# Pinned queue orders, half tiles for the sums of a step by seven, and a fourth such step in twelve gate/up groups of a two-layer decoder trunk

## The chip, the cores and the metric

The kernel runs on one core of one Trainium2 chip. The metric is device time in microseconds (us) of one execution. The core's engines, as the profile names them, are PE (TensorE, matmuls; PEld is its weight load), DVE (VectorE), ACT (ScalarE), POOL (GpSimd) and SP (SyncE, which here only starts transfers). Each works through a queue of its own in order.

## The reference

A decoder trunk of two layers on 256 tokens of width 2048, all in float32:

```python
h = x                                              # (1, 256, 2048)
for i in range(2):
    hn = rmsnorm(h, norm_mix[i])
    if i % 2 == 0:
        mix = pool_mixer(hn, pool_w[0], pool_scale[0])
    else:
        mix = diff_attention(hn, w_qkv[0], ..., w_o[0], lambda_init)
    h = h + mix
    h = h + swiglu(rmsnorm(h, norm_ffn[i]), w_gate[i], w_up[i], w_down[i])
return rmsnorm(h, final_norm)

def swiglu(h, wg, wu, wd):
    return (jax.nn.silu(h @ wg) * (h @ wu)) @ wd   # 2048 -> 5632 -> 2048
```

Nearly all arithmetic is in the products with `w_gate`, `w_up`, `w_down`, `w_qkv` and `w_o`.

## The kernel before, in words

**Stages.** A pooling mixer (the first 42 us of the trace), the FFN of layer 0 (to about 755 us), attention (to about 1085 us), the FFN of layer 1, and a last normalization. An FFN takes its 11 gate/up groups of 512 columns in chunks of 4, 4 and 3 (`CHUNKS`); behind each chunk come two down groups (`o` of 0 and 1) that add the chunk's share to the residual `x_tok`.

**A group and its steps.** `group` computes a 256 x 1024 block of results: 512 gate and 512 up columns, or 1024 columns of another product. It sums over *pairs* of 128 input rows: 8 pairs in a gate/up group, 8 or 6 in a down group. A pair is one step: one 1 MB load of four 128 x 512 weight blocks (B12, B11, B22, B21) into `raw`, which has three buffers. Float32 weights and operands are each split into a high and a low half of type fp32r, and a product of two blocks is three matmuls: high x high, high x low, low x high. ACT casts `whi` from `raw`, and VectorE subtracts to get `wlo` (`halves`); these too have three buffers each. The results lie in PSUM, one bank each of 128 x 512.

**Plain steps and steps by seven.** A plain step multiplies 2 x 2 blocks by 2 x 2 blocks in eight products, 24 matmuls. A step by seven uses Strassen's scheme (in Winograd's form): seven products, 21 matmuls, with four sums of weight blocks T1 to T4 (`sums` makes `tsum` on VectorE), which are split in their turn: `thi` by ACT, `tlo` by VectorE (`sum_halves`). The operand's sums S1 to S4 are made once, when it is transposed (`pair`), in a tile of eight blocks instead of four. Block B12 itself is not needed by such a step, so `halves` leaves it out (128 x 1536 instead of 128 x 2048). `SEVEN` names the pairs that go by seven in gate/up groups, (2, 4, 6), and in each layer's first group (4, 6). Down groups, the attention's q/k, v and output groups have tables of their own. The q/k and v groups take their pairs in the order `LATE`, with 4, 2 and 6 next to each other; their sums' halves have two buffers (`bufs=2`). In the FFN they have one.

**End of a group.** `combined` adds the seven banks up (one chain of ACT copies and eight VectorE additions named `c`), the gate half goes through SiLU on ACT, and `pair` transposes the result into an operand `h` of the down groups. The next group's first matmuls, meanwhile, are already running.

**What sets the order.** The code is written as a program for one thread. A scheduler orders each engine's queue by program order and by its own model of the engines; in two places of the pooling stage `high_priority` with a negative number moves work behind. Semaphores between the engines are derived from the tiles.

The lines of the profile before that matter: L189 the matmuls of a group, L124 and L125 the casts and subtractions of weights, L130, L132, L133 the sums, L139 and L140 their halves, L211 to L220 `combined`, L252 to L277 the operand's halves, L354 and L368 the pooling's weights and matmuls, L392 and L393 the pooling's residual.

The cut that both versions keep, of one product:

```python
for x, y in ((ah, hi), (ah, lo), (al, hi)):
    left[b] -= 1
    nc.tensor.matmul(ps[b], x, y[:, block], start=first, stop=(left[b] == 0))
```

## Time and profile before

| | |
|---|---|
| median of 3 runs | 1837.09 us (1836.84 to 1837.28) |
| the profiled execution's own time | 1837.09 us |
| its span, first to last instruction | 1835.3 us |
| busy: PE, PEld | 1823.0 us (99%), 1492.3 us (81%) |
| busy: DVE, ACT | 1630.5 us (89%), 1048.7 us (57%) |
| matmuls of L189 | 7,530 |
| steps, and steps by seven | 328 with a load, of them 114 by seven |
| loaded from HBM | 353 MB, 193 GB/s over the span |

How to read it: "busy" is the union of the times in which an engine had an instruction running. Matmuls overlap their neighbours, so one lasts 0.39 us in the records while the next starts 0.227 us after it; the pitch, not the duration, is what a matmul costs. A wait is written "waiter <- what it waited for". The clock column is the TensorE clock that was granted, 1.00 being full.

### The profile page before, as it was taken

How to read it: one execution, taken by the hardware profiler on the slowest of the kernel's cores; microseconds unless marked ns; L12 is line 12 of the kernel's file. 1: busy time of each engine (PE TensorE's matmuls, PEld its weight loads, DVE VectorE, ACT ScalarE, POOL GpSimd, SP SyncE). 2: the span in 40 equal slices, each digit the busy share in tenths (PEclk: the TensorE clock that was granted, in tenths of full speed). 3: DMA queues.
4: the chain of work that ended last, by engine and by line, in shares of the span. 5: the costliest groups of instructions: out<-in, count | busy, mean ns of one | idle time of the engine just before them, and what ended most of it. 6: DMA issues, size and time to landing. Idle time of an engine off the chain costs nothing.

```text
span 1835.3 us, 20926 instructions
## 1 busy us (share of the span) xinstructions
PE 1823.0 (99%) x8192; PEld 1492.3 (81%) x8192; DVE 1630.5 (89%) x1692; ACT 1048.7 (57%) x1026; POOL 0.7 (0%) x6
## 2 busy tenths in 40 slices
PE   9999999999999999999999999999999999999997
PEld 6888888888888888888888888888888888888886
DVE  7999999889899899989988789889899899988986
ACT  6655544555554556666667665555554555555563
POOL 0000000000000000000000000000000000000000
PEclk9999999999999999999999999999999999999999
DMA  7555555555555555544554555555555545556552
GB/s 271 200 184 193 208 196 209 204 187 205 205 194 197 205 184 184 206 173 174 182 183 163 181 184 184 206 185 205 204 190 202 207 183 193 212 215 210 202 189 110
DMA packets 50930, 356.35 MB, mean 194 GB/s; under 512 B 6160, under 2 KB 6288, under 8 KB 8464
## 3 DMA queue, kind: packets, MB, share of 16 engines
q1 hardware_dynamic: 49968, 353.40, 53.5%
q10 hardware_dynamic: 864, 1.63, 0.2%
q8 instruction: 64, 1.05, 0.2%
q14 instruction: 34, 0.28, 0.0%
HBM read 352.90 MB, written 2.10 MB: 193 GB/s over the span
## 4 chain that ended last, share of the span: by engine, by line
PE 97%; DVE 1%; ACT 1%; DMA 0%; issue 0%; SPq 0%; DVEq 0%; ACTq 0%
PE b L189 93%; PE b L259 2%; PE b L576 1%; PE b L607 0%; DMA x_tok<-x_n 0%; PE b L368 0%; PE b L624 0%; PE b L622 0%; PE b L623 0%; PE b L561 0%; DVE wlo L354 0%; DVE xt_hl L252 0%; ACT sq L240 0%; DVE wlo L125 0%; DVE z L392 0%
## 5 line engine op out<-in xcount | busy, mean ns | idle before, releaser
L189 PE MATMUL b<-whi,xp 128*128 128x512 f32 x2784 | 899.4, 392 | 0.0
L124 ACT CAST whi<-raw 128x1536 fp32r<-128x1536 f32 (+1 forms) x328 | 578.7, 1764 | 549.6 <-PE b L189 450.4
L125 DVE TENSOR_TENSOR wlo<-raw,whi 128x1536 fp32r<-128x1536 f32 (+1 forms) x328 | 689.6, 2103 | 159.2 <-ACT whi L124 158.9
L189 PEld LDWEIGHTS b<-whi,xp 128*128 128x128 f32 x2784 | 520.1, 188 | 108.2 <-ACT e L272 0.4
L189 PE MATMUL b<-wlo,xp 128*128 128x512 f32 x1392 | 544.2, 391 | 0.0
L189 PE MATMUL b<-whi,h 128*128 128x512 f32 x1108 | 354.2, 390 | 0.0
L189 PEld LDWEIGHTS b<-wlo,xp 128*128 128x128 f32 x1392 | 261.5, 188 | 53.0
L140 DVE TENSOR_TENSOR tlo<-tsum,thi 128x2048 fp32r<-128x2048 f32 x114 | 260.6, 2286 | 8.3 <-ACT thi L139 8.3
L189 PEld LDWEIGHTS b<-whi,h 128*128 128x128 f32 x1108 | 207.5, 188 | 43.2
L139 ACT CAST thi<-tsum 128x2048 fp32r<-128x2048 f32 x114 | 217.6, 1908 | 19.7 <-DVE tsum L133 17.2
L189 PE MATMUL b<-thi,xp 128*128 128x512 f32 x640 | 223.4, 389 | 0.0
L189 PE MATMUL b<-wlo,h 128*128 128x512 f32 x554 | 215.8, 389 | 0.0
L130 DVE TENSOR_TENSOR tsum<-raw 128x1024 f32<-128x1024 f32 x114 | 139.1, 1220 | 2.1 <-DMA raw<-w_v 0.6
L189 PEld LDWEIGHTS b<-thi,xp 128*128 128x128 f32 x640 | 120.1, 188 | 24.7
L189 PE MATMUL b<-tlo,xp 128*128 128x512 f32 x320 | 125.9, 393 | 0.0
L189 PEld LDWEIGHTS b<-wlo,h 128*128 128x128 f32 x554 | 104.0, 188 | 21.3
L189 PE MATMUL b<-thi,h 128*128 128x512 f32 x240 | 83.7, 390 | 0.0
L133 DVE TENSOR_TENSOR tsum<-tsum,raw 128x512 f32<-128x512 f32 x114 | 78.5, 689 | 2.2
L132 DVE TENSOR_TENSOR tsum<-tsum,raw 128x512 f32<-128x512 f32 x114 | 78.1, 685 | 0.6
L189 PEld LDWEIGHTS b<-tlo,xp 128*128 128x128 f32 x320 | 60.0, 188 | 16.5 <-DVE tlo L140 4.4
L189 PE MATMUL b<-whi,oT 128*128 128x512 f32 x216 | 69.7, 395 | 0.0
L189 PEld LDWEIGHTS b<-thi,h 128*128 128x128 f32 x240 | 45.0, 188 | 9.5 <-ACT thi L139 0.4
(147 smaller groups left out, 1211.7 us busy)
## 6 DMA issues: line engine op xcount, KB each, us to landing
raw<-w_gu SPq DMA_DIRECT2D x176, 1024.0 KB, 4.8
raw<-w_down SPq DMA_DIRECT2D x88, 1024.0 KB, 4.8
raw<-w_qk SPq DMA_DIRECT2D x32, 1024.0 KB, 4.8
raw<-w_v SPq DMA_DIRECT2D x16, 1024.0 KB, 4.8
raw<-w_o SPq DMA_DIRECT2D x16, 1024.0 KB, 4.8
x_tok<-x_n SPq DMA_DIRECT2D x4, 512.0 KB, 6.9
w<-pool_w SPq DMA_DIRECT2D x4, 512.0 KB, 7.5
raw<-pool_w SPq DMA_DIRECT2D x2, 1024.0 KB, 11.1
```

Of the source, the lines that this page charges most:

```text
L124: nc.scalar.copy(hi[:, lo_block:], raw[:, lo_block:])
L125: nc.vector.tensor_tensor(lo[:, lo_block:], raw[:, lo_block:], f32(hi[:, lo_block:]), ALU.subtract)
L130: nc.vector.tensor_tensor(t[:, T1:T3 + 1], raw[:, B11:B22 + 1], raw[:, B12:B12 + 1].broadcast_to([P, 2, 512]), ALU.add)
L132: nc.vector.tensor_tensor(t[:, T2], t[:, T1], raw[:, B22], ALU.add)
L133: nc.vector.tensor_tensor(t[:, T4], t[:, T2], raw[:, B21], ALU.add)
L139: nc.scalar.copy(hi, t)
L140: nc.vector.tensor_tensor(lo, t, f32(hi), ALU.subtract)
L189: nc.tensor.matmul(ps[b], x, y[:, block], start=first, stop=(left[b] == 0))
L259: nc.tensor.transpose(ps[:, i, 1 - t if seven else t], src(i, t), ident)
L576: nc.tensor.matmul(sc[:, :nk], qk[:, 0, c, qb * P:(qb + 1) * P], qk[:, 1, c, :nk], start=True, stop=True)
```

## The change

It does four things.

1. **More steps by seven.** `GATE_UP` lists the pairs for each layer and group. In 12 of the 22 gate/up groups (1, 3, 4, 5, 8 and 9 of each layer, counted from 0) pair 5 goes by seven as well, so that pairs 4, 5 and 6 do so one behind the other. The first group of layer 1 gets pair 2. `SEVEN` itself becomes (2, 4, 5, 6), so pair 5's operand has eight blocks everywhere; plain steps read four of them.
2. **Half tiles.** `tsum`, `thi` and `tlo` of 128 x 2048 become two tiles each of 128 x 1024: number 0 holds T1 and T3, number 1 holds T2 and T4. Each half is cast, subtracted and released by itself. All groups have one buffer of each half now, those of attention too.
3. **Order inside a step by seven.** If the next step is one by seven too, the products with the sums come first, half 0 then half 1, and those with B11, B21 and B22 behind; else the other way round.
4. **Pinned queue orders.** At the end of the program `in_order_of_need` builds a graph of all instructions, walks it as a list schedule with a table of latencies (for TensorE, VectorE, ACT, transfers and signals), ranks VectorE's and ACT's instructions by the latest time at which TensorE's use of them allows, and fixes the resulting order of the PE, DVE, ACT and SP queues by dependencies without a semaphore.

Where the instructions stand on an engine, before and now. Line numbers differ between the versions: L189 became L380, L125 became L314, L130, L132 and L133 became L319 to L321, L140 became L328, L252, L354, L392 and L393 became L443, L545, L583 and L584. Numbers behind names are of single tiles.

First place, VectorE in the second gate/up group of layer 0. The raw tiles 961, 996, 1026, 1061 hold pairs 4 to 7 before, 980, 1020, 1060, 1100 now. Before:

```order
L140 TENSOR_TENSOR tlo_972<-tsum_963,thi_971 128x2048
L130 TENSOR_TENSOR tsum_1028<-raw_1026 128x1024
L125 TENSOR_TENSOR wlo_1033<-raw_1026,whi_1032 128x1536
L132 TENSOR_TENSOR tsum_1028<-tsum_1028,raw_1026 128x512
L133 TENSOR_TENSOR tsum_1028<-tsum_1028,raw_1026 128x512
L125 TENSOR_TENSOR wlo_1064<-raw_1061,whi_1063 128x2048
L140 TENSOR_TENSOR tlo_1037<-tsum_1028,thi_1036 128x2048
L125 TENSOR_TENSOR wlo_1134<-raw_1131,whi_1133 128x2048
```

and now:

```order
L328 TENSOR_TENSOR tlo1_996<-tsum1_983,thi1_995 128x1024
L320 TENSOR_TENSOR tsum1_1023<-tsum0_1022,raw_1020 128x512
L321 TENSOR_TENSOR tsum1_1023<-tsum1_1023,raw_1020 128x512
L314 TENSOR_TENSOR wlo_1068<-raw_1060,whi_1067 128x1536
L328 TENSOR_TENSOR tlo0_1032<-tsum0_1022,thi0_1031 128x1024
L328 TENSOR_TENSOR tlo1_1036<-tsum1_1023,thi1_1035 128x1024
L319 TENSOR_TENSOR tsum0_1062<-raw_1060 128x1024
L314 TENSOR_TENSOR wlo_1103<-raw_1100,whi_1102 128x2048
L320 TENSOR_TENSOR tsum1_1063<-tsum0_1062,raw_1060 128x512
L328 TENSOR_TENSOR tlo0_1072<-tsum0_1062,thi0_1071 128x1024
L321 TENSOR_TENSOR tsum1_1063<-tsum1_1063,raw_1060 128x512
L314 TENSOR_TENSOR wlo_1173<-raw_1170,whi_1172 128x2048
```

Pair 5's sums and halves have come in between those of pairs 4 and 6; its `tlo0` (1032) stands behind pair 6's `wlo` (1068), and the next row after these is pair 6's `tlo1`, 1076, behind the next group's first `wlo` (1173).

Second place, TensorE at the end of the same group, from pair 6 (`xp_89`) to pair 7 (`xp_90`); `b` and a number is a PSUM bank. Before:

```order
L189 MATMUL b5_848<-thi_1036,xp_89 128x512
L189 MATMUL b5_848<-tlo_1037,xp_89 128x512
L189 MATMUL b5_848<-thi_1036,xp_89 128x512
L189 MATMUL b6_834<-whi_1063,xp_90 128x512
L189 MATMUL b6_834<-wlo_1064,xp_90 128x512
```

and now:

```order
L380 MATMUL b6_848<-whi_1102,xp_90 128x512
L380 MATMUL b6_848<-wlo_1103,xp_90 128x512
L380 MATMUL b1_943<-thi1_1075,xp_89 128x512
L380 MATMUL b5_862<-thi1_1075,xp_89 128x512
L380 MATMUL b6_848<-whi_1102,xp_90 128x512 x2
L380 MATMUL b6_848<-wlo_1103,xp_90 128x512
L380 MATMUL b6_848<-whi_1102,xp_90 128x512
L380 MATMUL b4_855<-whi_1102,xp_90 128x512
L380 MATMUL b4_855<-wlo_1103,xp_90 128x512
L380 MATMUL b4_855<-whi_1102,xp_90 128x512
L380 MATMUL b1_943<-tlo1_1076,xp_89 128x512
```

Matmuls of pair 7 have moved in between pair 6's with `thi1` and its first with `tlo1`.

Third place, TensorE at the first step by seven (pair 2) of layer 0's third group. Before:

```order
L189 MATMUL b6_1137<-whi_1201,xp_85 128x512
L189 MATMUL b1_1216<-thi_1205,xp_85 128x512
L189 MATMUL b2_1220<-thi_1205,xp_85 128x512
L189 MATMUL b3_1224<-thi_1205,xp_85 128x512
L189 MATMUL b4_1144<-whi_1201,xp_85 128x512
L189 MATMUL b1_1216<-tlo_1206,xp_85 128x512
```

and now:

```order
L380 MATMUL b6_1176<-whi_1241,xp_85 128x512
L380 MATMUL b4_1183<-whi_1241,xp_85 128x512
L380 MATMUL b4_1183<-wlo_1242,xp_85 128x512
L380 MATMUL b4_1183<-whi_1241,xp_85 128x512
L380 MATMUL b3_1263<-thi0_1245,xp_85 128x512
L380 MATMUL b3_1263<-tlo0_1246,xp_85 128x512
```

The three products with B22 (bank 4) now stand ahead of those with the sums. On VectorE, in the same place, before:

```order
L125 TENSOR_TENSOR wlo_1237<-raw_1234,whi_1236 128x2048
L277 TENSOR_TENSOR h_1109<-e_1115,h_1109 128x1024
L140 TENSOR_TENSOR tlo_1206<-tsum_1197,thi_1205 128x2048
L125 TENSOR_TENSOR wlo_1271<-raw_1264,whi_1270 128x1536
L130 TENSOR_TENSOR tsum_1266<-raw_1264 128x1024
```

and now:

```order
L321 TENSOR_TENSOR tsum1_1237<-tsum1_1237,raw_1234 128x512
L328 TENSOR_TENSOR tlo0_1246<-tsum0_1236,thi0_1245 128x1024
L468 TENSOR_TENSOR h_1148<-e_1154,h_1148 128x1024
L328 TENSOR_TENSOR tlo1_1250<-tsum1_1237,thi1_1249 128x1024
L314 TENSOR_TENSOR wlo_1281<-raw_1278,whi_1280 128x2048
```

The plain step's `wlo` and the transposed operand `h` stood ahead of the `tlo`; now the first half is ahead of both.

The diff, cut:

```diff
-SEVEN = (2, 4, 6)
+SEVEN = (2, 4, 5, 6)
+GATE_UP = [[(4, 6), (2, 4, 5, 6), (2, 4, 6), (2, 4, 5, 6), (2, 4, 5, 6), ...], [(2, 4, 6), (2, 4, 5, 6), ...]]
...
+SIGNAL = {PE: 54, DVE: 36, ACT: 36, SP: 36, POOL: 36}
+AGAIN = 70
+SETTLES = {DVE: 36, ACT: 120}
...
+def in_order_of_need(tc):
+    steps = steps_of(list(tc.nc.cur_bb.bb.instructions))
+    rank = [float(s.k) for s in steps]
+    start, end = walk(steps, rank)
+    for _ in range(ROUNDS):
+        limit = due(steps, start)
+        rank = [float(s.k) if s.engine in (PE, SP) else limit[s.k] for s in steps]
+        again, span = walk(steps, rank)
+        if span < end:
+            start, end = again, span
+    order = mybir.DependencyInfo(mybir.DependencyClass.NoSync, mybir.DependencyReason.DATA)
+    for e in (PE, DVE, ACT, SP):
+        line = sorted((s for s in steps if s.engine == e), key=lambda s: start[s.k])
+        for one, two in zip(line, line[1:]):
+            tc.add_manual_dep(two.ins, one.ins.name, order, reason="order of need")
+    return start, end, steps
...
     def sums(pool, raw):
-        t = pool.tile([P, 4, 512], F32, name="tsum")
-        nc.vector.tensor_tensor(t[:, T1:T3 + 1], raw[:, B11:B22 + 1],
-                                raw[:, B12:B12 + 1].broadcast_to([P, 2, 512]), ALU.add)
-        nc.vector.tensor_tensor(t[:, T2], t[:, T1], raw[:, B22], ALU.add)
-        nc.vector.tensor_tensor(t[:, T4], t[:, T2], raw[:, B21], ALU.add)
-        return t
+        s, t = (pool.tile([P, 2, 512], F32, name=f"tsum{i}") for i in range(2))
+        nc.vector.tensor_tensor(s, raw[:, B11:B22 + 1], raw[:, B12:B12 + 1].broadcast_to([P, 2, 512]), ALU.add)
+        nc.vector.tensor_tensor(t[:, 0], s[:, 0], raw[:, B22], ALU.add)
+        nc.vector.tensor_tensor(t[:, 1], t[:, 0], raw[:, B21], ALU.add)
+        return s, t

-    def sum_halves(pool, t, bufs):
-        hi = pool.tile([P, 4, 512], F32R, name="thi", bufs=bufs)
-        lo = pool.tile([P, 4, 512], F32R, name="tlo", bufs=bufs)
+    def sum_halves(pool, t, bufs, i):
+        hi = pool.tile([P, 2, 512], F32R, name=f"thi{i}", bufs=bufs)
+        lo = pool.tile([P, 2, 512], F32R, name=f"tlo{i}", bufs=bufs)
         nc.scalar.copy(hi, t)
         nc.vector.tensor_tensor(lo, t, f32(hi), ALU.subtract)
...
-            if seven:
-                plan.append([(M1, [(A11, 0, B11)]), (M2, [(A12, 0, B21)]), (M6, [(S2, 1, T2)]), (M7, [(S3, 1, T3)]),
-                             (P5, [(S1, 1, T1)]), (P3, [(S4, 0, B22)]), (P4, [(A22, 1, T4)])])
+            if seven and n + 1 < len(steps) and steps[n + 1][1]:
+                plan.append([(P5, [(S1, 1, 0)]), (M7, [(S3, 1, 1)]), (M6, [(S2, 2, 0)]), (P4, [(A22, 2, 1)]),
+                             (M1, [(A11, 0, B11)]), (M2, [(A12, 0, B21)]), (P3, [(S4, 0, B22)])])
+            elif seven:
+                plan.append([(M1, [(A11, 0, B11)]), (M2, [(A12, 0, B21)]), (P3, [(S4, 0, B22)]), (P5, [(S1, 1, 0)]),
+                             (M7, [(S3, 1, 1)]), (M6, [(S2, 2, 0)]), (P4, [(A22, 2, 1)])])
...
-                    by_seven = SEVEN if g else SEVEN[1:]
+                    by_seven = GATE_UP[layer][g]
...
-            cs = combined(group([(xp[p], p in by_seven, w_qk[g, p]) for p in order], hq, bufs=2), hq)
+            cs = combined(group([(xp[p], p in by_seven, w_qk[g, p]) for p in order], hq, bufs=1), hq)
...
     ffn(1, xq, ss_next, None, None)
+    in_order_of_need(tc)
```

The rest of the diff gives the last stage's `y` tiles two tiles per row block instead of one, in the places of the halves of `tsum` and `thi`.

More of the change, by code (lines that the diff above doesn't have):

```diff
@@ new lines, in walk @@
+def walk(steps, rank):
+    missing = [len(s.before) for s in steps]
+    ready, start = [0.0] * len(steps), [0.0] * len(steps)
+    engines = (PE, DVE, ACT, SP, POOL)
+    free, wire = {e: 0.0 for e in engines}, 0.0
+    known, count = {e: {} for e in engines}, {e: 0 for e in engines}
+    place = [0] * len(steps)
+    able, coming = {e: [] for e in engines}, {e: [] for e in engines}
+    for s in steps:
+        if not s.before:
+            heapq.heappush(coming[s.engine], (0.0, s.k))
+    for _ in steps:
+        now, e = min((free[e] if able[e] else max(free[e], coming[e][0][0]), i)
+                     for i, e in enumerate(engines) if able[e] or coming[e])
+        e = engines[e]
+        while coming[e] and coming[e][0][0] <= now:
+            k = heapq.heappop(coming[e])[1]
+            heapq.heappush(able[e], (rank[k], k))
+        s = steps[heapq.heappop(able[e])[1]]
+        waits = {}
+        for k in s.before:
+            t = steps[k].engine
+            if place[k] > max(waits.get(t, 0), known[e].get(t, 0)) and (t != e or e != PE):
+                waits[t] = place[k]
+        known[e].update(waits)
+        count[e] += 1
+        place[s.k] = count[e]
+        if len(waits) > 1 and ready[s.k] > free[e]:
+            now += AGAIN
+        start[s.k], free[e] = now, now + s.holds
+        end = now + s.lasts
+        if s.dma:
+            begin = max(now + s.holds, wire)
+            wire = begin + s.share
+            end = begin + s.lasts
+        for k in s.after:
+            t = steps[k].engine
+            if t != e or s.dma:
+                at = end + SIGNAL[t]
+            elif e == DVE or e == ACT and s.k in steps[k].reads:
+                at = end + SETTLES[e]
+            else:
+                at = now + s.holds
+            ready[k] = max(ready[k], at)
+            missing[k] -= 1
+            if not missing[k]:
+                heapq.heappush(coming[steps[k].engine], (ready[k], k))
+    return start, max(free.values())
@@ new lines, in due @@
+def due(steps, start):
+    by_start = sorted(steps, key=lambda s: start[s.k])
+    at, clock = {}, 0.0
+    for s in by_start:
+        if s.engine == PE:
+            at[s.k], clock = clock, clock + s.holds
+    limit = [0.0] * len(steps)
+    for s in reversed(by_start):
+        limit[s.k] = min([limit[k] - s.lasts - SIGNAL[steps[k].engine] for k in s.after] + [at.get(s.k, clock)])
+    return limit
+def in_order_of_need(tc):
[14 more added lines that the diff above has]
+    return start, end, steps
@@ L150, in group @@
         plan = []
[L151 to L154 removed]
+        for n, (a, seven, src) in enumerate(steps):
+            if seven and n + 1 < len(steps) and steps[n + 1][1]:
[4 more added lines that the diff above has]
+                             (M7, [(S3, 1, 1)]), (M6, [(S2, 2, 0)]), (P4, [(A22, 2, 1)])])
             else:
@@ L168, in prepared @@
             if seven:
-                w.append(sum_halves(pool, t, bufs))
+                w += [sum_halves(pool, t[i], bufs, i) for i in range(2)]
             return w
@@ L513, in ffn @@
                             if b == 0 and t == 0:
-                                ys.append([hp.tile([P, 2, 2, 512], F32, name="y", tag=("tsum", "thi")[i]) for i in range(2)])
-                                ys = ys[0]
-                            nc.vector.tensor_tensor(ys[o][:, t, b], x_at(t, j * 512),
+                                ys.extend([hp.tile([P, 2, 512], F32, name="y", tag=f"{n}{i}") for i in range(2)]
+                                          for n in ("tsum", "thi"))
+                            nc.vector.tensor_tensor(ys[o][t][:, b], x_at(t, j * 512),
                                                     final_sb[o][:, b * 512:(b + 1) * 512], ALU.mult)
@@ L617, in trunk_kernel @@
             order, by_seven = LATE if g else EARLY
-            cs = scaled(combined(group([(xp[p], p in by_seven, w_v[g, p]) for p in order], op_, bufs=2), op_), (r_col, r_col))
+            cs = scaled(combined(group([(xp[p], p in by_seven, w_v[g, p]) for p in order], op_, bufs=1), op_), (r_col, r_col))
             for h in range(4 * g, 4 * g + 4):
@@ L636, in trunk_kernel @@
         for g in range(2):
-            cs = combined(group([(oT[p], p in SEVEN_O, w_o[g, p]) for p in range(NP)], op_, bufs=2), op_)
+            cs = combined(group([(oT[p], p in SEVEN_O, w_o[g, p]) for p in range(NP)], op_, bufs=1), op_)
             for b in range(2):
```

110 lines of the change are left out of this document (102 added, 8 removed).

## The prediction

> **What bounds the kernel now.** I read the busy shares first, then the chain that ended last, then the waits, then stretches and single rows of one gate/up group.
>
> ```profile
> PE 1823.0 (99%) x8192; PEld 1492.3 (81%) x8192; DVE 1630.5 (89%) x1692; ACT 1048.7 (57%) x1026; POOL 0.7 (0%) x6
> PE 97%; DVE 1%; ACT 1%; DMA 0%; issue 0%; SPq 0%; DVEq 0%; ACTq 0%
> 135.28 41.38 PE b L189 x181
> 177.99 41.42 PE b L189 x181
> 220.75 124.33 PE b L189 x547
> 135.30:178.00 42.70, 42.70 (x192) 35.00 (x192) 38.84 (x36) 24.16 (x21) 0.00 (x0) 1.00 0.54 197
> 263.50:346.40 82.90, 82.90 (x371) 68.63 (x371) 75.11 (x64) 42.96 (x29) 0.00 (x0) 1.00 0.60 216
> ```
>
> The chain is 97% TensorE. The third chain row gives the matmul's pitch: 124.33 / 547 = 0.2273 us, at full clock (the 1.00 of the windows). Consecutive gate/up groups begin at 135.28 and 177.99, 42.71 us apart. VectorE is the second: in that group it is busy 38.84 of 42.70 us, and in the two down groups behind the first chunk 75.11 of 82.90. So a matmul less is worth its pitch, but only while VectorE keeps up, and it has 3.9 us to spare in a gate/up group.
>
> ```profile
> ACT whi L124 <- PE b L189: 450.4, 206, 4.0
> DVE wlo L125 <- ACT whi L124: 158.9, 131, 3.1
> PEld b L189 <- DVE tlo L140: 6.9, 17, 0.4
> 143.56 0.84 PE L189 MATMUL b<-thi,xp 128*128 128x512 f32 x3
> 144.24 0.39 PE L189 MATMUL b<-whi,xp 128*128 128x512 f32 x1
> 144.62 0.50 PE L189 MATMUL b<-tlo,xp 128*128 128x512 f32 x1
> 144.96 0.39 PE L189 MATMUL b<-thi,xp 128*128 128x512 f32 x1
> ```
>
> The waits (total, times, longest) tell who is ahead. In 206 of 328 steps ACT waits for TensorE to free a `whi`: the preparation stands at its full lead of three buffers. TensorE waits for preparation 17 times, all for `tlo`. The PE rows show one: starts 144.24, 144.62, 144.96, so two pitches took 0.72 instead of 0.45, a loss of 0.27 us.
>
> ```profile
> 191.44 2.28 DVE L125 TENSOR_TENSOR wlo<-raw,whi 128x2048 fp32r<-128x2048 f32 x1
> 193.65 2.28 DVE L140 TENSOR_TENSOR tlo<-tsum,thi 128x2048 fp32r<-128x2048 f32 x1
> 197.13 1.76 DVE L125 TENSOR_TENSOR wlo<-raw,whi 128x1536 fp32r<-128x1536 f32 x1
> 198.80 0.69 DVE L132 TENSOR_TENSOR tsum<-tsum,raw 128x512 f32<-128x512 f32 x1
> 210.56 1.22 DVE L130 TENSOR_TENSOR tsum<-raw 128x1024 f32<-128x1024 f32 x1
> 211.69 0.68 DVE L213 TENSOR_TENSOR c<-b,c 128x512 f32<-128x512 f32 x1
> 212.29 0.68 DVE L212 TENSOR_TENSOR c<-b,c 128x512 f32<-128x512 f32 x1
> 212.89 0.68 DVE L215 TENSOR_TENSOR c<-c,c 128x512 f32<-128x512 f32 x1
> L276 ACT CAST h<-e 128x1024 fp32r<-128x1024 f32 x16 | 16.7, 1044 | 0.0
> L139 ACT CAST thi<-tsum 128x2048 fp32r<-128x2048 f32 x114 | 217.6, 1908 | 19.7 <-DVE tsum L133 17.2 <-PE b L189 2.5
> ```
>
> From start to start a VectorE instruction costs about 0.08 us less than it lasts: 2.21 us at 2048 columns (191.44 to 193.65), 1.67 at 1536, 1.13 at 1024, 0.60 at 512.
>
> **The change part by part.**
>
> *More steps by seven.* A pair step takes 24 matmuls, a step by seven 21. Pair 5 goes by seven in 12 groups, and layer 1's first group gains pair 2 (it had 4 and 6): 13 steps, 39 matmuls of 7,530, 39 x 0.2273 = 8.9 us off TensorE's path. On VectorE each costs one `tsum` of 1024 (1.13) and two of 512 (1.20), two half `tlo` (2.26), less 2.21 - 1.67 for `B12`, no longer split: 4.05 us, 53 us in all. On ACT it is two casts of 1.04 less the shorter `whi`, about 1.7 us; ACT at 57% hides it. Two more pair-5 operands and their sums are a few short instructions per layer, beside the down-projection or attention matmuls.
>
> *Half tiles.* The 114 old steps trade one `tlo` of 2.21 for two of 1.13: 0.05 to 0.07 each, 6 to 8 us more VectorE work over the kernel; on ACT 2 x 1.044 for 1.908, 0.18 each. VectorE's total becomes about 1630 + 53 + 8 = 1691 us of some 1825, 93%.
>
> The Trainium skill ("VectorE: DVE Perf Modes", The DRAIN you can't avoid) says that the next operation does not start until the pipe is empty, and adds that one which is not held starts earlier. By the first half of that rule the 0.08 us of overlap would be gone from each of the 44 or so VectorE instructions of a four-seven group: an estimate of 43.2 (worked out below) + 3.5 = 46.7 us instead of 41.8, and 12 such groups would put the kernel at some 1885 us. I give it no chance of its own: in this trace 512-column operations start 0.60 apart and last 0.68, so the second half holds here.
>
> *Does VectorE keep up?* A four-seven group asks 38.84 + 4.05 + 4 x 0.07 = 43.2 us of VectorE; TensorE's share of it is 42.71 - 0.68 - 0.27 = 41.8. VectorE falls 1.4 us behind in each. A three-seven group leaves 42.4 - 39.1 = 3.3, a down group (82.90 - 75.11) / 2 = 3.9. At most two four-seven groups stand side by side (4 and 5 of a layer), so 2.8 us of lead is needed, and the lead is two steps, 2 x 24 x 0.2273 = 10.9 us. I count the totals as covered.
>
> *The tight place* is inside such a group: pairs 4, 5 and 6 by seven in a row, with one `thi`/`tlo` buffer each. The first place shown under the change is VectorE's queue there. Where one `tlo` stood between plain steps, pair 5's halves now stand behind pair 6's `wlo`. Count from pair 4's first matmul. `thi0` is free after 6 matmuls (1.36), its cast takes 1.04, its `tlo0` 1.22: 3.6 us at the earliest, wanted by pair 5's second matmul at 22 x 0.2273 = 5.0. But VectorE also has `tlo1_996`, two sums and `wlo_1068` ahead of it: 1.13 + 1.20 + 1.67 + 1.22 = 5.2. It is on time only if VectorE starts that row 0.2 us before pair 4 does, which its inputs allow (`thi1` was last read by pair 2). `tlo1_1036`, at about 6.3, is wanted at 28 x 0.2273 = 6.4. The slack is a tenth or two.
>
> Next comes `tlo1_1076`, pair 6's, which stands behind the next group's first `wlo` (2.2 us). The second place shows TensorE's queue, which would want it there. Nine or so of pair 7's matmuls (`xp_90`) fill the 2 us in which `tlo1` is late. TensorE loses nothing while VectorE is within that.
>
> Attention's `LATE` groups have the same run (4, 2, 6), now with one buffer instead of two: 4 groups. With the 12 that is 16 groups, two boundaries each, 32. No row shows such a boundary. Nearest from above is today's wait, 0.4; from below 0, the arithmetic just done. I take 0.1, since the count came out level, not late: 3.2 us (0 to 12.8).
>
> *The wait that goes.* Today's `tlo` wait stands at the first step by seven of a group. The third place shows it in layer 0's third group. P3 comes ahead of the sums, and the first `tlo0` is a half, ready 1.1 us sooner; on VectorE it no longer stands behind the transposed operand's 1.22 us or pair 3's `wlo`. All but one of the 17 waits lie at such a place, once in a group: 16 x 0.27 = 4.3 us, which I take whole (bounds 0 and 4.3). Late next there is nothing: `tlo1` has six matmuls more.
>
> *The pinned order elsewhere.* In the pooling start TensorE idles for VectorE, and one row of its chain is the first `wlo` of the FFN:
>
> ```profile
> 28.98 0.74 DVE z L392
> 29.73 2.20 DVE wlo L125
> 31.92 0.60 DVE x_tok L393
> 32.52 0.79 DVE xt_hl L252 x2
> ```
>
> That `wlo` now stands behind the last pooling halves, but the pooling's own `wlo_291` (2.2 us) has moved in behind `z_280`. I take 1.0 us gained (0 to 2.2); late next are the transposes and L368 behind them. The tail behind the last matmul keeps its chain. SP keeps its loads in order, one a step; each 1 MB lands in 4.8 us (below) beside three raw buffers, so 0. Two more ACT table loads, 1.3 us each, fall in attention and are hidden by ACT's 43% idle; without that cover they cost 2.6.
>
> ```profile
> raw<-w_gu SPq DMA_DIRECT2D x176, 1024.0 KB, 4.8
> ```
>
> *Sum*, on the profiled span: 1835.3 - 8.9 - 4.3 - 1.0 + 3.2 = 1824.3. The execution's time was 1837.09, 1.8 above its span and equal to the median: 1826.1, rounded to 1826.5.
>
> **The rivals.**
>
> *The ring binds* (result within 0.2%). If each of the 32 boundaries costs today's wait, 0.4, that is 12.8 instead of 3.2: 1836. For it: the slack of a tenth or two, and queues that run strictly in order, so one late `whi` delays both halves. Against: TensorE has other matmuls to put in.
>
> *VectorE becomes the bound* (slower). If the lead is not carried from group to group, because single `thi` and `tsum` buffers stop VectorE from running ahead, each four-seven group lasts VectorE's 43.2 instead of 41.8: 12 x 1.4 = 17 us more, 1843. It decides from the point where over 10.6 of these 17 us are uncovered. For it: 43.2 is over even the old 42.7. Against: the 206 waits at full lead.
>
> *The order gives more*: ring free, all 2.2 us of the start: 1822.
>
> *The change does not do what it says* is excluded for the count: the built order has 39 matmuls fewer.
>
> **How the numbers follow.** Forecast (1822.5 to 1833) 0.60, ring 0.17, VectorE 0.11, more 0.09, something else slower 0.03. A measurement of this kernel tells 0.2%, 3.7 us, from no change. Faster is the forecast, the order giving more, and a little of the ring: 0.72; same 0.15; slower 0.13. The range runs from 1821.5 (all gains, no loss) to 1837.5, the ring at its upper price.
>
> **What would show it.** Right: 7,491 matmuls on the product line; a four-seven group some 41.8 us from the next; VectorE at 93%; the wait of TensorE on `tlo` gone from the first step by seven. Wrong: TensorE waiting on `tlo0` or `tlo1` at pairs 5 and 6 (ring), or four-seven groups 43 us long with no idle VectorE in them (bound).

## The result, and the profile after

| | before | after |
|---|---|---|
| median | 1836.96 us (1836.77 to 1837.28, 4 runs) | 1821.74 us (1821.4 to 1821.8, 4 runs) |
| ratio | | 0.9917, 95% interval 0.9899 to 0.9934 |
| span of the profiled execution | 1835.3 us | 1819.9 us |

The change takes 15.2 us off. The forecast was 1826.5, with a range from 1821.5 to 1837.5: the side is right, and the time lies at the lower end of the range, below the band from 1822.5 to 1833 that was given 0.60.

The busy shares, and the shares of the chain that ended last:

```profile
PE 1806.3 (99%) x8153; PEld 1487.6 (82%) x8153; DVE 1686.3 (93%) x1875; ACT 1084.0 (60%) x1170; POOL 0.7 (0%) x6
PE 98%; DVE 1%; ACT 1%; issue 0%; DVEq 0%; ACTq 0%
```

TensorE has 39 instructions fewer (8,192 before; the profile before stands in the prediction) and VectorE 55.8 us more work, 93% of the span.

Layer 0's groups 1, 2 and 3 and the first down group, each window from its first product matmul to that of the next:

```profile
85.71:127.43 41.72, 41.72 (x189) 34.57 (x188) 40.36 (x41) 25.01 (x22) 0.00 (x0) 1.00 0.54 197
127.43:169.92 42.49, 42.49 (x192) 35.10 (x191) 41.09 (x41) 24.57 (x22) 0.00 (x0) 1.00 0.55 199
169.92:211.77 41.85, 41.85 (x189) 34.49 (x188) 40.64 (x42) 25.91 (x24) 0.00 (x0) 1.00 0.55 200
211.77:254.19 42.42, 42.42 (x192) 35.11 (x191) 41.19 (x43) 23.59 (x21) 0.00 (x0) 1.00 0.54 199
```

The columns behind the length are the busy times of PE, PEld, VectorE, ACT and POOL. The groups with pairs 2, 4, 5 and 6 by seven, "four-seven groups" from here on (first and third row), last 41.72 and 41.85 us, and TensorE is busy in all of it. By the prediction's count VectorE needs 43.2 us for such a group. It does 40.4 to 40.6 of it there, and the rest falls into the next group, whose VectorE time rises from 38.84 (before) to 41.1.

The waits (total, times, longest), and two rows of the page's groups (busy, mean ns of one, idle before):

```profile
ACT whi L313 <- PE b L380: 270.4, 146, 5.5
DVE wlo L314 <- ACT whi L313: 68.4, 47, 3.7
DVE c L402 <- PE b L380: 17.2, 17, 1.3
PEld b L380 <- DVE c L408: 2.9, 11, 0.5
```

```profile
L328 DVE TENSOR_TENSOR tlo<-tsum,thi 128x1024 fp32r<-128x1024 f32 x254 | 306.5, 1216 | 2.3 <-ACT thi L327 2.0
L380 PEld LDWEIGHTS b<-tlo,xp 128*128 128x128 f32 x372 | 69.8, 188 | 15.1
```

TensorE's 17 waits for `tlo` are gone: the idle time before the weight loads from `tlo`, 15.1 us over 372, has no releaser. ACT waits for TensorE 146 times instead of 206, and at 270 instead of 450 us: the preparation is less far ahead. TensorE's new wait is for `c` L408, the addition that frees bank 4 at a group's end; the trace before has one such wait, of 0.2 us.

To say where the 15 us are, I matched every matmul of the trace to its step by the built order. Lengths are from a group's first product matmul to the next group's; "loss" is what exceeds the count of matmuls times 0.2273 us and the transposes between.

```
us                              before   after    change
first product matmul             41.76   38.67     -3.1
layer 0, group 0                 46.18   47.04     +0.9
12 four-seven groups, a mean     42.2    41.5      -8.4 in all
layer 1, group 0 (pair 2 added)  43.64   43.16     -0.5
other gate/up and down groups                      -2.7
attention                       378.04  376.51     -1.5
last matmul                    1825.61 1810.31    -15.3
```

Attention here is its eight groups, the two output groups among them; before, it ends at 1124.29 us, not at the 1085 of the stage list.

The start shows its cause best in the chain. Before, its rows from 17.9 to 34.5 us were VectorE's and ACT's; now they are TensorE's only; four of those from 18 to 48 us:

```profile
18.90 5.61 PE b L559 x24
26.77 2.81 PE b L559 x12
33.72 3.74 PE b L559 x16
45.02 2.98 PE b L380 x13
```

### The profile page after: what moved, and what is told of

The parts are those of the page before. It is cut to its first block, busy times and chain, and to the rows that moved or that the text cites. A ratio compares the mean times of both kernels' runs of the same rounds, so it can differ in the third digit from the quotient of the medians.

```text
span 1819.9 us, 21122 instructions
## 1 busy us (share of the span) xinstructions
PE 1806.3 (99%) x8153; PEld 1487.6 (82%) x8153; DVE 1686.3 (93%) x1875; ACT 1084.0 (60%) x1170; POOL 0.7 (0%) x6
## 4 chain that ended last, share of the span: by engine, by line
PE 98%; DVE 1%; ACT 1%; issue 0%; DVEq 0%; ACTq 0%
PE b L380 92%; PE b L450 2%; PE b L559 1%; PE b L555 1%; PE b L767 1%; PE b L798 0%; DVE wlo L314 0%; PE b L813 0%; PE b L485 0%; PE b L814 0%; PE b L530 0%; PE b L815 0%; DVE c L402 0%; DVE c L403 0%; PE b L752 0%
## 5 line engine op out<-in xcount | busy, mean ns | idle before, releaser
L380 PE MATMUL b<-whi,xp 128*128 128x512 f32 x2654 | 850.3, 392 | 0.4 <-ACT xp L467 0.3
L314 DVE TENSOR_TENSOR wlo<-raw,whi 128x1536 fp32r<-128x1536 f32 (+1 forms) x328 | 681.3, 2077 | 69.6 <-ACT whi L313 68.4
L380 PEld LDWEIGHTS b<-whi,xp 128*128 128x128 f32 x2654 | 496.4, 188 | 104.9 <-DVE c L408 2.7
L380 PE MATMUL b<-wlo,xp 128*128 128x512 f32 x1327 | 520.1, 392 | 0.1
L327 ACT CAST thi<-tsum 128x1024 fp32r<-128x1024 f32 x254 | 266.3, 1052 | 183.9 <-DVE tsum L321 96.1
L380 PE MATMUL b<-whi,h 128*128 128x512 f32 x1108 | 349.2, 390 | 0.0
L328 DVE TENSOR_TENSOR tlo<-tsum,thi 128x1024 fp32r<-128x1024 f32 x254 | 306.5, 1216 | 2.3 <-ACT thi L327 2.0
L380 PEld LDWEIGHTS b<-wlo,xp 128*128 128x128 f32 x1327 | 249.2, 188 | 50.9 <-DVE wlo L314 0.5
L380 PE MATMUL b<-thi,xp 128*128 128x512 f32 x744 | 248.4, 390 | 0.0
L380 PEld LDWEIGHTS b<-whi,h 128*128 128x128 f32 x1108 | 207.6, 188 | 42.6 <-DVE c L408 0.2
L380 PE MATMUL b<-wlo,h 128*128 128x512 f32 x554 | 216.0, 390 | 0.1
L380 PEld LDWEIGHTS b<-thi,xp 128*128 128x128 f32 x744 | 139.4, 188 | 28.8 <-ACT thi L327 0.2
L319 DVE TENSOR_TENSOR tsum<-raw 128x1024 f32<-128x1024 f32 x127 | 154.5, 1216 | 0.6
L380 PE MATMUL b<-tlo,xp 128*128 128x512 f32 x372 | 144.9, 389 | 0.0
L380 PEld LDWEIGHTS b<-wlo,h 128*128 128x128 f32 x554 | 104.0, 188 | 21.9 <-DVE wlo L314 0.5
L320 DVE TENSOR_TENSOR tsum<-tsum,raw 128x512 f32<-128x512 f32 x127 | 86.7, 683 | 0.6
L321 DVE TENSOR_TENSOR tsum<-tsum,raw 128x512 f32<-128x512 f32 x127 | 86.7, 682 | 0.5
L380 PEld LDWEIGHTS b<-tlo,xp 128*128 128x128 f32 x372 | 69.8, 188 | 15.1
L380 PE MATMUL b<-thi,h 128*128 128x512 f32 x240 | 78.7, 389 | 0.0
L677 ACT ACTIVATE c<-c,r_tok 128x512 f32<-128x512 f32 x44 | 31.9, 724 | 63.1 <-DVE c L403 36.1
L380 PE MATMUL b<-whi,oT 128*128 128x512 f32 x216 | 69.0, 395 | 0.0
```

The costliest lines, as they stand in the source:

```text
L314: nc.vector.tensor_tensor(lo[:, lo_block:], raw[:, lo_block:], f32(hi[:, lo_block:]), ALU.subtract)
L319: nc.vector.tensor_tensor(s, raw[:, B11:B22 + 1], raw[:, B12:B12 + 1].broadcast_to([P, 2, 512]), ALU.add)
L320: nc.vector.tensor_tensor(t[:, 0], s[:, 0], raw[:, B22], ALU.add)
L321: nc.vector.tensor_tensor(t[:, 1], t[:, 0], raw[:, B21], ALU.add)
L327: nc.scalar.copy(hi, t)
L328: nc.vector.tensor_tensor(lo, t, f32(hi), ALU.subtract)
```

## The experiments

Group 0.6 is group 6 of layer 0. Where a run changes the program, the pinned orders are worked out anew for it.

### The parts, one at a time

**The pinned order left out.**

```diff
     ffn(1, xq, ss_next, None, None)
-    in_order_of_need(tc)
```

> The changed kernel without the pinned queue orders; half tiles, the new order inside a step and all 13 further steps by seven stay. Theory A (the pinned order is what lets three steps by seven in a row run with one buffer, and it also shortened the start): the start gives back its 2 to 3 us, attention 1.5, and the 32 boundaries between neighbouring steps by seven cost up to 0.4 us each: about 1830 to 1838 us. Theory B (half tiles and the order inside a step are enough, the queue orders matter only in the start): 1824 to 1826 us, with no wait of TensorE on the halves of the sums.

Measured: 1838.29 us (1837.75 to 1839.45), ratio 1.0007 (0.9997 to 1.0016), just past the upper end of theory A. Without the pin the rest of the change gains nothing: 16.5 us lie between it and the full change. The start is back at 41.64 us, 3.0 later, and the FFNs are 6.6 and 6.2 us longer, most of it in and behind the four-seven groups (1.6 us in 0.9). TensorE's largest wait is for bank 4, once in the group behind each of the twelve; the other two, for the halves of the sums, are the ring that the prediction feared:

```profile
PEld b L380 <- DVE c L408: 9.6, 12, 1.0
PEld b L380 <- ACT thi L327: 4.4, 16, 0.4
PEld b L380 <- DVE tlo L328: 4.3, 16, 0.6
```

**The fourth steps left out** (the old table, half tiles and pin kept).

```diff
-SEVEN = (2, 4, 5, 6)
-GATE_UP = [[(4, 6), (2, 4, 5, 6), ...], [(2, 4, 6), ...]]
+SEVEN = (2, 4, 6)
+GATE_UP = [[(4, 6)] + [(2, 4, 6)] * 10, [(4, 6)] + [(2, 4, 6)] * 10]
```

> The changed kernel with the old table of steps by seven (39 matmuls back); half tiles, order inside a step and pinned queues stay. Theory A (a matmul less is worth its full pitch, VectorE has lead to spare): 1821.7 + 39 x 0.2273 = 1830.6 us. Theory B (VectorE at 93% already takes some of the gain): the 53 us less of VectorE work give something back, 1827 to 1829.5 us. VectorE should be busy about 1686 - 53 = 1633 us.

Measured: 1827.13 us (1826.95 to 1827.42), ratio 0.9946 (0.9931 to 0.9961). The 13 steps bring 5.4 us, not 8.9 (theory B). The missing 3.5 us have places: 0.6 in group 0.0, where one pair's operand is larger; 0.36 each in 0.6 and 1.6; 0.45 each in 1.2 and the down group behind 1.3; 0.15 each in 0.10 and 1.10; 0.8 in the second q/k group.

**The pinned order alone**, on the kernel before (full tiles, old table).

```diff
 # the kernel before
     ffn(1, xq, ss_next, None, None)
+    in_order_of_need(tc)
```

> The kernel before with its queue orders pinned by the same planner, nothing else changed (full tiles, 3 steps by seven, two buffers of sums in attention). Theory A (the 6.5 us beside the matmuls come from the queue orders): about 1830.5 us. Theory B (the orders give only the start, 2 us; the waits on the low half of the sums went because the tiles are halved and the products with the raw blocks come first): 1833 to 1835 us, with the 0.3 us losses at the first step by seven still there.

Measured: 1829.33 us (1828.92 to 1829.54), ratio 0.9957 (0.9942 to 0.9972): 7.8 us from order alone. The start is 2.8 us earlier, and in the FFNs all the losses of 0.3 us are gone: they fall by 2.3 and 2.1 us. So the `tlo` wait goes by order; the half tiles aren't needed for it. They and the new order of products are enough too: in the run without the pin, groups 0.7 and 1.7 and the down groups behind them, which follow no four-seven group, last 42.44 to 42.45 us instead of 42.72 to 42.77. Either removes the wait.

**The fourth steps alone**, with full tiles, one buffer of them in attention as well, and no pin.

```diff
 # the kernel before
-SEVEN = (2, 4, 6)
+SEVEN = (2, 4, 5, 6)
+GATE_UP = [[(4, 6), (2, 4, 5, 6), ...], ...]
...
-                    by_seven = SEVEN if g else SEVEN[1:]
+                    by_seven = GATE_UP[layer][g]
...
-            cs = combined(group([(xp[p], p in by_seven, w_qk[g, p]) for p in order], hq, bufs=2), hq)
+            cs = combined(group([(xp[p], p in by_seven, w_qk[g, p]) for p in order], hq, bufs=1), hq)
```

> The kernel before with the new table of steps by seven alone: full tiles of the sums with one buffer (in attention too, since a second does not fit beside the larger operand), old order inside a step, no pinned queues. Theory A (neighbouring steps by seven then wait for the turnover of the one buffer: a cast of 1.9 us and a subtraction of 2.3 us, less the 7 to 10 matmuls that need no sums, so 2 to 2.7 us at each of 24 boundaries in the FFNs and 8 in attention): 1837 - 8.9 + 32 x 2 to 2.7 = 1892 to 1914 us. Theory B (the scheduler fills the wait with matmuls of the next plain step): 1828 to 1841 us.

Measured: 1898.85 us (1896.96 to 1900.52), ratio 1.0339 (1.0322 to 1.0356), theory A. A four-seven group lasts 44.4 to 48.1 us.

**Full tiles, with the fourth steps and the pin.** With the full tiles this run also takes the old order of products inside a step back, so it does not price the tiles alone; full tiles with the sums first were not run.

```diff
 # the changed kernel
-    def sum_halves(pool, t, bufs, i):
-        hi = pool.tile([P, 2, 512], F32R, name=f"thi{i}", bufs=bufs)
-        lo = pool.tile([P, 2, 512], F32R, name=f"tlo{i}", bufs=bufs)
+    def sum_halves(pool, t, bufs):
+        hi = pool.tile([P, 4, 512], F32R, name="thi", bufs=bufs)
+        lo = pool.tile([P, 4, 512], F32R, name="tlo", bufs=bufs)
...
-            if seven and n + 1 < len(steps) and steps[n + 1][1]:
-                plan.append([(P5, ...), (M7, ...), (M6, ...), (P4, ...), (M1, ...), (M2, ...), (P3, ...)])
-            elif seven:
-                plan.append([(M1, ...), (M2, ...), (P3, ...), (P5, ...), (M7, ...), (M6, ...), (P4, ...)])
+            if seven:
+                plan.append([(M1, ...), (M2, ...), (M6, ...), (M7, ...), (P5, ...), (P3, ...), (P4, ...)])
```

> The changed kernel, with the kernel before's full tiles of 128x2048 for the sums and their halves, one buffer of each in attention too, with the fourth steps and the pinned order. Theory A: from the last matmul that reads a full tile to the next step's first that needs it are some 9 matmuls, 2.05 us, while its cast takes 1.9 and its subtraction 2.3, so each boundary between neighbouring steps by seven lacks 2 us, less what the pinned order fills in: 1860 to 1895. Theory B: the pinned order finds other matmuls for the gap, as it does for the halves: 1822 to 1835.

Measured: 1899.0 us (1898.0 to 1900.93), ratio 1.0338 (1.0324 to 1.0352): the pin adds up to nothing against the run before (it brings 3.2 us at the start and loses as much behind it), and both theories' numbers are too low. The places are theory A's. In group 0.1 TensorE stands 1.97 us at pair 6's first `thi` and 1.30 at its first `tlo` (beyond the pitch), and then something comes on top that no theory had. Windows around that place (the column behind POOL is the granted clock):

```profile
115.00:124.00 9.00, 9.00 (x41) 7.33 (x40) 8.93 (x6) 3.90 (x3) 0.00 (x0) 1.00 0.56 204
126.00:128.20 2.20, 1.20 (x4) 0.67 (x4) 2.13 (x1) 1.84 (x2) 0.00 (x0) 1.00 0.82 328
128.20:130.00 1.80, 1.59 (x5) 1.25 (x6) 0.85 (x2) 0.00 (x0) 0.00 (x0) 0.69 0.80 332
130.00:132.00 2.00, 2.00 (x6) 1.57 (x5) 1.97 (x3) 0.99 (x2) 0.00 (x0) 0.50 0.09 37
132.00:134.00 2.00, 2.00 (x10) 1.63 (x9) 2.00 (x2) 0.71 (x2) 0.00 (x0) 0.93 0.00 0
```

Behind the two stops the clock is 0.50 for some three microseconds. Matmuls start 0.43 us apart there, as two rows of TensorE's queue show:

```profile
129.49 0.63 PE L378 MATMUL b<-thi,xp 128*128 128x512 f32 x1
129.92 0.63 PE L378 MATMUL b<-tlo,xp 128*128 128x512 f32 x1
```

Seven of them lose 0.20 us each. 1.97 + 1.30 + 1.4, and 0.4 in those at the edges, are the group's 5.1 us over its count. The Trainium skill ("TensorE: Matmul & The Clock Gate", Part 1) has the clock fall to half after an idle window of about 3.4 us; here it fell though neither gap was that long, 1.97 and 1.30 us with four matmuls between.

**The products with the sums never first.**

```diff
 # the changed kernel
-            if seven and n + 1 < len(steps) and steps[n + 1][1]:
-                plan.append([(P5, ...), (M7, ...), (M6, ...), (P4, ...), (M1, ...), (M2, ...), (P3, ...)])
-            elif seven:
+            if seven:
                 plan.append([(M1, ...), (M2, ...), (P3, ...), (P5, ...), (M7, ...), (M6, ...), (P4, ...)])
```

> The changed kernel, with the products with B11, B21 and B22 first in every step by seven, also where the next step is one by seven too (no sums first). Theory A: the lists of latencies reorder the matmuls anyway, and between the last use of a half and the first use of the next step's same half lie 15 matmuls (3.4 us) in both forms, so the time is within 1 us of 1821.74. Theory B: with the sums last in pairs 4 and 5 their halves come free a step too late, and each boundary of a four-seven group loses 0.3 us or more: 24 boundaries and 8 in attention, 1830 or more.

Measured: 1839.64 us (1839.47 to 1840.08), ratio 1.0014 (1.0006 to 1.0023). Theory A is wrong: this order is worth 17.9 us, more than the whole change brings. Theory B has the sum (1830 or more), but not the place. The losses lie at the start of the group behind: 2.0 us in 0.6, 0.10, 1.6, 1.10 and in the down groups behind 0.3 and 1.3, and 0.9 to 1.2 in 0.2, 0.5, 0.9, 1.5 and 1.9; attention is 1.6 us longer. The waits:

```profile
ACT thi L327 <- PE b L377: 47.2, 33, 3.2
PEld b L377 <- DVE wlo L314: 12.6, 6, 2.1
```

The first was 19.8 us over 20 times in the changed kernel; the second, six of up to 2.1 us, is TensorE waiting for a plain `wlo`. VectorE's rows before the down group behind 0.3 say why, here and then in the changed kernel (that group starts at 212.6 here, at 211.8 there):

```profile
211.01 0.69 DVE L399 TENSOR_TENSOR c<-b,c 128x512 f32<-128x512 f32 x1 [1.19 <-PE b L377]
211.73 0.69 DVE L400 TENSOR_TENSOR c<-b,c 128x512 f32<-128x512 f32 x1
212.34 0.68 DVE L401 TENSOR_TENSOR c<-b,c 128x512 f32<-128x512 f32 x1
213.12 0.69 DVE L403 TENSOR_TENSOR c<-c,c 128x512 f32<-128x512 f32 x1
213.73 2.29 DVE L314 TENSOR_TENSOR wlo<-raw,whi 128x2048 fp32r<-128x2048 f32 x1
```

```profile
206.19 1.21 DVE L328 TENSOR_TENSOR tlo<-tsum,thi 128x1024 fp32r<-128x1024 f32 x1
208.34 0.69 DVE L402 TENSOR_TENSOR c<-b,c 128x512 f32<-128x512 f32 x1 [0.94 <-PE b L380]
```

The additions of `combined` start 1.6 us before the next group here, 3.4 us there. Pair 5's halves are read last instead of first, nine matmuls (2.05 us) later; so pair 6's halves, the last products with them, and the additions that wait for those are late. The bank they free is late, TensorE's order goes to the next step's first product instead, and that step's `wlo` (213.73) stands in VectorE's queue behind the additions.

**Attention's Exp behind its square root**, against the two extra table loads.

```diff
-        nc.scalar.activation(le, l_ps[:, 0:2], AF.Exp)
+        nc.vector.tensor_scalar(small[:, 16:17], r_col[:, 0:1], 0.0, None, ALU.mult)
+        nc.scalar.activation(le, l_ps[:, 0:2], AF.Exp, bias=small[:, 16:17])
```

> The changed kernel, with a zero bias for attention's Exp that is worked out behind the square root, so that ACT's table loads fall from 9 to 7 again (one VectorE instruction on a single column more). Theory A: the first q/k group's loss of 0.7 to 0.8 us is the extra table load ahead of that group's operand work, and it goes: that group lasts some 47.0 instead of 47.74 us and the kernel 0.7 us less, 1820.5 to 1821.5 against 1821.74. Theory B: the load lies beside ACT's idle time, as the prediction had it, and the loss is the order's: the group stays at 47.7 and the time within 0.3 us.

Measured: 1820.93 us (1820.84 to 1821.15), ratio 0.9912 (0.9899 to 0.9926). Theory A: the second q/k group (the expectation calls it the first) lasts 46.83 instead of 47.74 us, and the rest of the kernel stays as it was to 0.2 us a stage. ACT's queue in the changed kernel and TensorE's weight load behind it, then ACT's queue here:

```profile
791.05 1.28 ACT L774 ACT_TABLE_LOAD   x1
794.10 0.57 ACT L800 COPY qk<-b 128x512 f32<-128x512 f32 x1
794.72 0.95 PEld L767 LDWEIGHTS b<-qk 128*128 128x128 f32 x6 [1.08 <-ACT qk L800]
```

```profile
792.90 0.57 ACT L801 COPY qk<-b 128x512 f32<-128x512 f32 x1
```

The load itself met no wait, but the copy of `qk` stands behind it, and TensorE waited 1.08 us for that copy. It comes 1.2 us earlier now, and TensorE's longest wait for `qk` in the kernel is 0.2 us.

### How many such steps VectorE can carry

**Pair 0 instead of pair 5**, so that no three steps by seven stand in a row.

```diff
-SEVEN = (2, 4, 5, 6)
+SEVEN = (0, 2, 4, 6)      # and (0, 2, 4, 6) in the 12 groups of GATE_UP
```

> The changed kernel with the further step by seven at pair 0 instead of pair 5 (pairs 0, 2, 4, 6), so that no two steps by seven are neighbours in a gate/up group; same count of matmuls. Theory A (the run 4, 5, 6 costs nothing any more with halves and pinned queues; what is left of 3.5 us of losses comes from VectorE falling behind over a whole group): same losses or, as pair 0 falls together with the end-of-group additions, more: 1821 to 1827 us. Theory B (the run itself costs the 3.5 us): 1818 us.

Measured: 1825.51 us (ratio 0.9937, 0.9919 to 0.9955), 3.8 us worse. Theory B is out: without a run of three nothing is gained. By place, 2.1 us of it lie in attention, where the edit changes no step, 0.8 in the start, and the FFNs together are 0.7 longer. In them the losses in 0.6, 1.6, 1.2 and behind 1.3 are gone, and others stand in 0.1 (0.9), 1.1 (1.5) and behind 0.3 (0.7). What made attention longer wasn't found.

**A fourth step in 20 of the 22 groups.**

```diff
+GATE_UP = [[(4, 6)] + [(2, 4, 5, 6)] * 10, [(2, 4, 6)] + [(2, 4, 5, 6)] * 10]
```

> The changed kernel with the fourth step in 20 instead of 12 gate/up groups (all but the first of each layer): 24 matmuls fewer, 34 us more VectorE work. Theory A (VectorE falls 1.4 us behind in each such group and has lead for two or three in a row; then it is the bound, and a group lasts its 43.2 us): groups behind the second four-seven one in a row last 42.5 to 43.2, the further groups bring nothing: 1821 to 1827 us. Theory B (VectorE keeps up): 1821.7 - 24 x 0.2273 = 1816.3 us.

Measured: 1840.13 us, ratio 1.0016 (1.0007 to 1.0026). Here is the prediction's rival, VectorE as the bound. Groups 0.5, 0.6 and 0.7, the second, third and fourth four-seven group in a row, and a wait:

```profile
341.00:382.80 41.80, 41.80 (x189) 34.41 (x188) 40.30 (x39) 24.69 (x22) 0.00 (x0) 1.00 0.55 200
382.80:426.20 43.40, 42.15 (x190) 34.57 (x189) 43.01 (x44) 25.62 (x25) 0.00 (x0) 1.00 0.54 195
426.20:469.40 43.20, 42.02 (x189) 34.53 (x188) 43.06 (x44) 25.93 (x25) 0.00 (x0) 1.00 0.52 192
```

```profile
PEld b L380 <- DVE wlo L314: 23.9, 16, 2.1
```

The second lasts 41.80, as in the changed kernel; the third and fourth last 43.4 and 43.2, with VectorE busy in 43.0 and 43.1 of them, and TensorE waits for a plain `wlo` 16 times. The 43.2 us worked out beforehand for VectorE are there. Theory A has this, but its sum, 1821 to 1827, is far too low; among others, the down groups behind the chunks last 1.0 to 2.1 us longer than in the changed kernel, which it didn't count.

**Fourth steps in groups 1, 3, 5, 8 and 10 only**, never two neighbours (10 groups).

```diff
-GATE_UP = [[(4, 6), (2, 4, 5, 6), (2, 4, 6), (2, 4, 5, 6), (2, 4, 5, 6), (2, 4, 5, 6), (2, 4, 6), (2, 4, 6), (2, 4, 5, 6), (2, 4, 5, 6), (2, 4, 6)], ...]
+GATE_UP = [[(4, 6), (2, 4, 5, 6), (2, 4, 6), (2, 4, 5, 6), (2, 4, 6), (2, 4, 5, 6), (2, 4, 6), (2, 4, 6), (2, 4, 5, 6), (2, 4, 6), (2, 4, 5, 6)], ...]
```

> The changed kernel with the fourth step in 10 groups that are never side by side inside a chunk of gate/up groups (1, 3, 5, 8, 10 of each layer): 6 matmuls more than the change, 1.4 us. Theory A (the waits at the start of the groups that follow two four-seven groups are VectorE's debt): those 0.3 to 0.4 us losses go where two stood side by side, 1822 to 1822.5 us. Theory B (the losses come behind any four-seven group): as many losses as such groups, 1823 us or more.

Measured: 1822.32 us (ratio 0.9919, 0.9903 to 0.9935). The loss of 0.3 in group 6 is gone, as theory A has it. There is one such step fewer in each layer, 1.4 us of matmuls, and the time is 0.6 us above the change's. The losses of 0.43 in group 1.2 and in the down group behind 1.3 stay. The trace of the changed kernel shows what they are, for 1.2 (which starts at 1199.47):

```profile
PEld b L380 <- DVE wlo L314: 1.1, 2, 0.5
1196.27 0.69 DVE L402 TENSOR_TENSOR c<-b,c 128x512 f32<-128x512 f32 x1 [1.06 <-PE b L380]
1199.00 2.28 DVE L314 TENSOR_TENSOR wlo<-raw,whi 128x2048 fp32r<-128x2048 f32 x1
1201.34 0.50 PE L380 MATMUL b<-wlo,xp 128*128 128x512 f32 x1
```

The two waits are one in each of these groups. The additions of `combined` start 3.2 us before the group, a plain `wlo` stands behind four of them, and TensorE waits 0.5 us for it. In 0.2, with the same order, they start 3.66 us before the group, and less than 0.1 is lost.

**A fourth step also in group 7**, on top of the later Exp (14 groups).

```diff
-GATE_UP = [[..., (2, 4, 6), (2, 4, 6), (2, 4, 5, 6), (2, 4, 5, 6), (2, 4, 6)], ...]
+GATE_UP = [[..., (2, 4, 6), (2, 4, 5, 6), (2, 4, 5, 6), (2, 4, 5, 6), (2, 4, 6)], ...]
```

> The changed kernel with attention's later Exp (1820.93), and a fourth step by seven also in gate/up group 7 of each layer, 14 such groups in all. Theory A: VectorE's slack decides. It idles 2.4 us in group 7 and 3.4 and 4.0 us in the two down groups behind it, so the 1.4 us that such a group lacks are made up there: both groups fall from 42.43 to about 41.8 us, no group behind them is longer, and the time is 1.2 to 1.4 us less, 1819.5 to 1819.8. Theory B: each four-seven group gives back about half of its gain in its successor, whatever stands there, as over the twelve (5.4 of 8.9 us were kept): 0.5 to 0.9 us less, 1820.0 to 1820.5.

Measured: 1824.22 us (1823.8 to 1824.33), ratio 0.9929 (0.9916 to 0.9943): 3.3 us above the run with the later Exp, against both theories. Group 7 itself is 0.68 us shorter, but the down group behind it grows from 42.43 to 44.26 us, in both layers. VectorE and TensorE there:

```profile
461.30 0.69 DVE L402 TENSOR_TENSOR c<-b,c 128x512 f32<-128x512 f32 x1 [1.33 <-PE b L380]
464.03 2.28 DVE L314 TENSOR_TENSOR wlo<-raw,whi 128x2048 fp32r<-128x2048 f32 x1
466.37 0.50 PE L380 MATMUL b<-wlo,h 128*128 128x512 f32 x1 [1.48 <-DVE wlo L314]
```

It is the wait of the run with the sums never first: the additions start 1.8 us before the next group (463.1), too late for its second step. So the 3.4 and 4.0 us of slack in the groups behind didn't help. In the changed kernel VectorE is busy 41.0 us in group 6 and 40.1 in group 7, where a three-seven group's own work is 39.1: group 7 still works off 1 us of what groups 4 and 5 left. Here it adds 1.4 of its own, and the additions come late. Past that point the loss isn't a few tenths but 1.8 us. Where a plain `wlo` stands behind four of the additions, as here, the measured cases are: additions 3.7 us before the next group, almost nothing lost; 3.2 us before it, 0.4; 1.6 to 1.8 us before it, 1.8 to 2.0.

**And in layer 1's first group** (15 groups).

```diff
-GATE_UP = [..., [(2, 4, 6), (2, 4, 5, 6), ...]]
+GATE_UP = [..., [(2, 4, 5, 6), (2, 4, 5, 6), ...]]
```

> As the run with group 7, and a fourth step by seven also in layer 1's first gate/up group, 15 such groups. Theory A: that group has no slack: VectorE idles 0.42 us in its 43.16 and a fourth step asks 4.05 us more, so VectorE sets its length, less what lead attention's last group leaves (4.2 us idle there): it or the next becomes longer, and the time is 0.5 to 3.5 us above the run with group 7. Theory B: a step by seven less is 0.68 us of TensorE wherever it stands: 0.5 to 0.7 us below that run.

Measured: 1827.81 us (1827.66 to 1828.7), ratio 0.9951 (0.9939 to 0.9964), 3.6 us above the last run: theory A, just past its upper end. That group and the next:

```profile
1115.40:1160.40 45.00, 43.15 (x198) 35.04 (x196) 44.23 (x58) 31.84 (x38) 0.00 (x0) 1.00 0.41 152
1160.40:1204.70 44.30, 42.41 (x188) 34.49 (x189) 43.04 (x43) 25.48 (x23) 0.00 (x0) 1.00 0.57 212
```

They lasted 43.16 and 41.81 us in the last run.

The best version seen is the changed kernel with the later Exp, 1820.93 us.

## Why the prediction was right, and where its sizes were off

The prediction had -11.0 us; the trace has -15.3 up to the last matmul. In its own terms:

| term | predicted | measured |
|---|---|---|
| 39 matmuls fewer | -8.9 | -8.9 |
| the `tlo` waits | -4.3 | -4.7 (the pin alone, in the FFNs behind group 0.0) |
| the start | -1.0 | -3.1 |
| group 0.0, with a larger operand | 0 | +0.9 |
| the ring | +3.2 | 0 at pairs 4 to 6 |
| new waits behind four-seven groups | 0 | +2.0, what is left (0.6, 1.6: 0.35 each; 1.2, behind 1.3: 0.45 each; 0.10, 1.10: 0.15 each) |
| attention | 0 | -1.5 |

The side and the largest term are earned. The nearness to a sum is luck: 1821.7, with no ring and 2.2 us of the start, is the rival "the order gives more", which was given 0.09, and the measured time meets it because terms that neither had cancel: 0.9 more at the start, 0.4 at the `tlo` waits and 1.5 in attention against 0.9 in group 0.0 and 2.0 of new waits.

- **Matmuls.** The count came out (7,491), the eight four-seven groups behind another gate/up group last 41.72 to 41.86 us as forecast (the four behind a down group, among whose matmuls no transposes fall, 40.80 to 40.82), and VectorE's total, 1686 us and 93%, is within 5 us of the forecast 1691.
- **The `tlo` wait.** The size was right, the reason only in part: I gave it to the half tile, the reordered products and the queue together. The pin alone removes it, and so do the other two without the pin. (The waits before were 17 for `tlo` and one for `thi`, not `tlo` alone.)
- **The ring** was the term that was most mis-sized. In the changed kernel's four-seven groups TensorE loses next to nothing at pairs 4 to 6 (one wait for `thi`, 0.2 us, in all), so the lower bound, 0, was the one to take. But the slack is easily lost: without the pin, without half tiles and their order of products, or with the other order of products alone the kernel is at 1838, 1899 and 1840 us. The prediction did the arithmetic from pair 4 to pair 5, where it came out level, and left pair 6 to the matmuls of pair 7. It did not count that with pair 5's sums first and pair 6's last, 24 matmuls instead of 15 lie between the last use of a half and the next step's first.
- **"I count the totals as covered"** is the step that was right by luck of place. The lead of two steps, 10.9 us, isn't there when it is needed: the additions at a group's end wait for TensorE's last matmuls (17 waits of VectorE, up to 1.3 us), and what stands behind them in VectorE's queue waits as well. Two four-seven groups side by side already cost 0.3 us in the next; one more, two groups on, costs 1.8 (group 7), and a row of them makes VectorE the bound. The rival's price of a group, 43.2 us, was right. What kept it away is the choice of twelve groups, at most two side by side; the prediction took that as enough for its lead, and it is just enough: two groups more cost 3.3 us.
- **Late next.** The prediction looked for what comes late next at the first step by seven and found nothing; nothing came late there. At the next group's start something did: bank 4, freed by `c` L408. At the start of group 0.6 the chain goes through the additions of group 0.5, the last of them L408, and TensorE starts 0.04 us behind that:

```profile
376.76 0.69 DVE c L403
379.50 0.61 DVE c L408
380.16 2.35 PE b L380 x9
```

- **The table loads** weren't hidden: 0.9 us of the 2.6. ACT's idle share is no cover when a copy that TensorE waits for stands behind the load.
- **The start** gained 3.1 us, more than its upper bound of 2.2 (2.8 by the pin alone), since not one `wlo` but the whole chain of VectorE and ACT there was taken off TensorE's path. Of the 0.9 us that group 0.0 gives back, 0.6 come with the fourth steps: the prediction had pair 5's larger operand beside the down-projection or attention, but layer 0's is made in the start, and in group 0.0 TensorE waits 0.7 us for an operand's cast, a wait that the run without fourth steps doesn't have.
- **Attention** was set to 0. The pin alone gives 0.3 us there; with the half tiles, one buffer of each and the new order of products it is 2.4, and the two table loads of the full change take 0.9 back. In the full change four of the eight groups gain 0.5 to 0.9 each, and I had costed those edits at nothing.
- **The rule on the empty pipe**, which the Trainium skill states ("VectorE: DVE Perf Modes", The DRAIN you can't avoid) and the prediction gave no chance, stays without one: by its first half VectorE would need an estimated 46.7 us for a four-seven group, and where VectorE set the length, in the run with 20 such groups, it took 43.2 to 43.6.
